# Row maxima of an 8192 x 8192 matrix: two rows a partition in each load, a finer tail, and a last store straight from the result tile

## The chip, the cores and the metric

One core of one Trainium2 chip. The metric is the device time in microseconds (us), the median of several executions. The profiled span is 1.84 us shorter than the measured time in the kernel before.

## The reference

```python
x = np.random.randn(8192, 8192).astype(np.float32)     # 268 MB
np.linalg.norm(x, ord=np.inf, axis=1)                  # max |x| of each row: 8192 results
```

Every byte is read once and little is computed, so the load stream sets the scale.

## The kernel before

A row block is 128 rows, one a partition. Each of 64 row blocks is loaded into one of five buffers and reduced on the vector engine (DVE). The last ten are cut into pieces whose partial maxima are combined by one more small reduction. At the end all results are transposed on the tensor engine (PE), copied out of the memory it writes to (PSUM) and stored.

```python
COOLDOWN = ([[4096, 4096]] * 7 + [[4096, 2048, 2048]]
            + [[2048] * 4] + [[2048, 2048, 1536, 1280, 1280]])
x_t = x.rearrange("(t p) m -> t p m", p=P)
pool = ctx.enter_context(tc.tile_pool(name="sbuf", bufs=5))
res = single.tile([P, T], mybir.dt.float32)
for t in range(T):
    xt = pool.tile([P, n_cols], x.dtype)
    for h, w in enumerate(chunks[t]):
        # ... dst is res[:, t] for a whole block, partial[:, h] for a piece
        nc.sync.dma_start(out=xt[:, off : off + w], in_=x_t[t, :, off : off + w])
        nc.vector.tensor_reduce(out=dst, in_=xt[:, off : off + w], axis=X,
                                op=max, apply_absolute_value=True)
    # ... if in pieces: tensor_reduce of partial[:, :n] into res[:, t]
nc.tensor.transpose(res_t_psum, res, ident)
nc.vector.tensor_copy(out=res_t, in_=res_t_psum)
nc.sync.dma_start(out=out.rearrange("(t p) -> t p", p=P), in_=res_t)   # 64 runs of 512 B
```

## Time and profile before

| | kernel before |
|---|---|
| time, median (range) | 634.71 us (634.56 to 634.78) |
| span | 632.9 us |
| loads, mean rate over the span | 80, 424 GB/s |
| vector engine busy | 88% |
| last byte of the input in | 626.4 us |
| last reduction ends | 629.3 us |
| last store: issued, issue to landing | 630.2, 1.8 us |

The prediction shows the lines for the rate, the end of the input and the last reduction. The last row is from the page's list of DMA issues (output and input, issuing queue, count, size of one, median us from issue to landing), followed by the wait of the sync queue at the end of the program (total, times, longest):

```profile
out_dram<-res_t SPq DMA_DIRECT2D x1, 32.0 KB, 1.8
```

```profile
SPq L107 <- DMA out_dram<-res_t: 1.1, 1, 1.1
```

### The profile page before, as it was taken

The page shows a single profiled execution, that of the slowest core. Times are in us where ns is not written, and L with a number is a line of the kernel's source. Part 1 is how long each engine was busy: PE and PEld are TensorE (multiplying, and loading weights), DVE is VectorE, ACT ScalarE, POOL GpSimd, SP SyncE. Part 2 cuts the span into 40 slices and gives each one's busy share as a digit, 9 for nine tenths or more (in the row PEclk, how much of TensorE's full clock was granted, in tenths as well). Part 3 has the DMA queues.
Part 4 walks back from the last instruction along what each step waited for, and adds up shares of the span by engine and source line. Part 5 has one row for each costly group of instructions (what it writes and reads, how often), then busy time and mean ns, then how long its engine had stood idle before and what let it go on. Part 6 is the DMA issues. An engine that isn't in the chain of part 4 may idle for free.

```text
span 632.9 us, 294 instructions
## 1 busy us (share of the span) xinstructions
PE 0.4 (0%) x1; PEld 0.1 (0%) x1; DVE 558.9 (88%) x91; POOL 0.7 (0%) x6
## 2 busy tenths in 40 slices
PE   0000000000000000000000000000000000000000
PEld 0000000000000000000000000000000000000000
DVE  1988988988989889889898898898988989999997
POOL 0000000000000000000000000000000000000000
DMA  8999999999999999999999999999999999999995
GB/s 373 439 437 437 433 431 433 431 431 431 431 431 431 431 431 431 431 431 431 431 431 431 431 431 431 431 431 431 431 437 433 435 435 418 427 428 431 425 421 219
DMA packets 11602, 268.49 MB, mean 424 GB/s; under 512 B 1296, under 2 KB 1360, under 8 KB 1744
## 3 DMA queue, kind: packets, MB, share of 16 engines
q1 hardware_dynamic: 11600, 268.47, 98.9%
q14 instruction: 2, 0.02, 0.0%
HBM read 268.44 MB, written 0.03 MB: 424 GB/s over the span
## 4 chain that ended last, share of the span: by engine, by line
DMA 75%; DVE 24%; SPq 0%; issue 0%; PE 0%; DVEq 0%
DMA xt<-in_x_dram 75%; DVE res L59 15%; DVE partial L59 8%; SPq L55 0%; DVE res L68 0%; PE res_t_psum L78 0%; DVE res_t L80 0%; DVEq L59 0%
## 5 line engine op out<-in xcount | busy, mean ns | idle before, releaser
L59 DVE TENSOR_REDUCE res<-xt 128x1 f32<-128x8192 f32 x54 | 469.0, 8686 | 67.6 <-DMA xt<-in_x_dram 67.6
L59 DVE TENSOR_REDUCE partial<-xt 128x1 f32<-128x4096 f32 (+3 forms) x26 | 88.1, 3430 | 2.7 <-DMA xt<-in_x_dram 2.6
L68 DVE TENSOR_REDUCE res<-partial 128x1 f32<-128x2 f32 (+3 forms) x10 | 1.6, 156 | 0.3
L80 DVE COPY res_t<-res_t_psum 64x128 f32<-64x128 f32 x1 | 0.3, 283 | 0.6 <-PE res_t_psum L78 0.6
L78 PE MATMUL res_t_psum<-ident,res 128*64 128x128 f32 x1 | 0.4, 393 | 629.5 <-DVE res L68 629.5
masks.py:199 POOL TENSOR_SCALAR_AFFINE_SELECT ident<-ident 128x128 f32<-128x128 f32 x1 | 0.3, 292 | 0.1
L78 PEld LDWEIGHTS res_t_psum<-ident,res 128*64 128x64 f32 x1 | 0.1, 128 | 629.4 <-issue 629.4
masks.py:197 POOL MEMSET ident<- 128x128 f32 x1 | 0.2, 204 | 0.3 <-POOLq L96 0.3
L96 POOL MEMSET const-bfloat16-1.0<- 128x1 bf16 x1 | 0.1, 101 | 0.0
L96 POOL MEMSET const-uint8-127<- 128x1 uint8 x1 | 0.1, 101 | 0.0
L96 POOL MEMSET const-float32-0.0<- 128x1 f32 x1 | 0.1, 98 | 0.2 <-issue 0.2
L96 POOL MEMSET const-float32-1.0<- 128x1 f32 x1 | 0.1, 98 | 0.0
## 6 DMA issues: line engine op xcount, KB each, us to landing
xt<-in_x_dram SPq DMA_DIRECT2D x54, 4096.0 KB, 39.8
xt<-in_x_dram SPq DMA_DIRECT2D x15, 2048.0 KB, 38.7
xt<-in_x_dram SPq DMA_DIRECT2D x8, 1024.0 KB, 28.3
xt<-in_x_dram SPq DMA_DIRECT2D x2, 640.0 KB, 17.9
xt<-in_x_dram SPq DMA_DIRECT2D x1, 768.0 KB, 19.3
out_dram<-res_t SPq DMA_DIRECT2D x1, 32.0 KB, 1.8
```

What stands on the lines that cost most here:

```text
L59: nc.vector.tensor_reduce(out=dst, in_=xt[:, off : off + w], axis=mybir.AxisListType.X, op=mybir.AluOpType.max, apply_absolute_value=True,)
L68: nc.vector.tensor_reduce(out=res[:, t : t + 1], in_=partial[:, : len(ch)], axis=mybir.AxisListType.X, op=mybir.AluOpType.max,)
L78: nc.tensor.transpose(res_t_psum, res, ident)
L80: nc.vector.tensor_copy(out=res_t, in_=res_t_psum)
L96: nc = _bacc.Bacc("TRN2", target_bir_lowering=False, num_devices=1)
```

## The change

The intent: fewer, larger loads where the stream is long (two rows of a partition are neighbours in memory, so a load moves 64 KB runs into a ring of columns); then pieces that shrink to 384 columns just as fast as the vector engine's lag may shrink, so that little is left when the last byte lands; the partial maxima lie behind the last piece in the ring, so that its reduction takes them along; and all results but the last 128 leave early, the last 128 without transpose and copy.

```diff
-    xt = pool.tile([P, n_cols], x.dtype)                 # five buffers of 8192 columns
+    ring = single.tile([P, RING + PAD], f32)             # RING = 3 * 16384 columns
+    x_big = x[:split].rearrange("(t p r) m -> t p (r m)", p=P, r=R)      # R = 2
+    for t in range(n_big):                               # 24 loads, 48 row blocks
+        nc.sync.dma_start(out=buf, in_=x_big[t])
+        absmax(res_big[:, t, :], buf.rearrange("p (r m) -> p r m", r=R))
+    for t, widths in enumerate(tail):                    # 16 row blocks; the last in 13 pieces
...
+            if i < n - 1:
+                absmax(ring[:, end + i : end + i + 1], ring[:, at : at + w])
+            else:
+                absmax(res_tail[:, t : t + 1], ring[:, at : at + w + n - 1])
+    store_early()                                        # all but the last 128, transposed
-    nc.tensor.transpose(res_t_psum, res, ident)
-    nc.vector.tensor_copy(out=res_t, in_=res_t_psum)
-    nc.sync.dma_start(out=out.rearrange("(t p) -> t p", p=P), in_=res_t)
+    nc.sync.dma_start(                                   # 128 runs of 4 B, side by side
+        out=out_tail[n_tail - 1].rearrange("(p o) -> p o", o=1),
+        in_=res_tail[:, n_tail - 1 : n_tail],
+    )
```

More of the change, by code (lines that the diff above doesn't have):

```diff
@@ L5, with tail_pieces @@
 import concourse.tile as tile
-from concourse import bass_utils, mybir
+from concourse import mybir
 from concourse.masks import make_identity
 from concourse._compat import with_exitstack
-COOLDOWN = (
-    [[4096, 4096]] * 7
-    + [[4096, 2048, 2048]]
-    + [[2048, 2048, 2048, 2048]]
-    + [[2048, 2048, 1536, 1280, 1280]]
-)
+P = 128
+R = 2
+RING = 3 * 16384
+PAD = 32
+LOAD = (1.1815e-3, 0.043)
+REDUCE = (1.0417e-3, 0.060)
+FIRST = 384
+GRAIN = 64
+def tail_pieces(n_cols, big):
+    slack = 0.0
+    lag = REDUCE[0] * FIRST + REDUCE[1]
+    rows = []
+    while True:
+        left, row = n_cols, []
+        while left:
+            w = FIRST if not rows and not row else int((lag + slack - REDUCE[1]) / REDUCE[0])
+            w = max(GRAIN, w // GRAIN * GRAIN)
+            if w >= left:
+                w = left
+            elif 2 * w > left:
+                w = (left // 2 + GRAIN - 1) // GRAIN * GRAIN
+            row.append(w)
+            left -= w
+            slack += (LOAD[0] - REDUCE[0]) * w + LOAD[1] - REDUCE[1]
+        rows.append(row[::-1])
+        if (lag + slack - REDUCE[1]) / REDUCE[0] > big:
+            return rows[::-1]
 @with_exitstack
@@ L26 @@
     nc = tc.nc
-    P = 128
+    f32 = mybir.dt.float32
     n_rows, n_cols = x.shape
-    assert n_rows % P == 0
-    T = n_rows // P
-    if n_cols == 8192 and T >= len(COOLDOWN):
-        chunks = [[n_cols]] * (T - len(COOLDOWN)) + COOLDOWN
-    else:
-        chunks = [[n_cols]] * T
-    x_t = x.rearrange("(t p) m -> t p m", p=P)
-    pool = ctx.enter_context(tc.tile_pool(name="sbuf", bufs=5))
-    single = ctx.enter_context(tc.tile_pool(name="single", bufs=1))
-    psum_pool = ctx.enter_context(tc.tile_pool(name="psum", bufs=1, space=bass.MemoryType.PSUM))
@@ L43 @@
-    res = single.tile([P, T], mybir.dt.float32)
-    maxch = max(len(c) for c in chunks)
-    if maxch > 1:
-        partial = single.tile([P, maxch], mybir.dt.float32)
-    for t in range(T):
-        ch = chunks[t]
-        assert sum(ch) == n_cols
-        xt = pool.tile([P, n_cols], x.dtype)
-        off = 0
-        for h, w in enumerate(ch):
-            dst = res[:, t : t + 1] if len(ch) == 1 else partial[:, h : h + 1]
-            nc.sync.dma_start(
-                out=xt[:, off : off + w],
-                in_=x_t[t, :, off : off + w],
-            )
-            nc.vector.tensor_reduce(
-                out=dst,
-                in_=xt[:, off : off + w],
-                axis=mybir.AxisListType.X,
-                op=mybir.AluOpType.max,
-                apply_absolute_value=True,
-            )
-            off += w
-        if len(ch) > 1:
-            nc.vector.tensor_reduce(
-                out=res[:, t : t + 1],
-                in_=partial[:, : len(ch)],
-                axis=mybir.AxisListType.X,
-                op=mybir.AluOpType.max,
-            )
@@ L75 @@
-    ident = single.tile([P, P], mybir.dt.float32)
-    make_identity(nc, ident)
-    res_t_psum = psum_pool.tile([T, P], mybir.dt.float32)
-    nc.tensor.transpose(res_t_psum, res, ident)
-    res_t = single.tile([T, P], mybir.dt.float32)
-    nc.vector.tensor_copy(out=res_t, in_=res_t_psum)
-    nc.sync.dma_start(out=out.rearrange("(t p) -> t p", p=P), in_=res_t)
+    tail = tail_pieces(n_cols, R * n_cols)
+    n_all = n_rows // P
+    if (n_all - len(tail)) % R:
+        tail.insert(0, [n_cols])
@@ new lines @@
+    n_big = (n_all - len(tail)) // R
+    n_tail = len(tail)
+    split = n_big * R * P
+    x_big = x[:split].rearrange("(t p r) m -> t p (r m)", p=P, r=R)
+    x_tail = x[split:].rearrange("(t p) m -> t p m", p=P)
+    out_tail = out[split:].rearrange("(t p) -> t p", p=P)
+    single = ctx.enter_context(tc.tile_pool(name="single", bufs=1))
+    psum_pool = ctx.enter_context(
+        tc.tile_pool(name="psum", bufs=1, space=bass.MemoryType.PSUM)
+    )
+    ring = single.tile([P, RING + PAD], f32)
@@ new lines, with room, absmax @@
+    ident = single.tile([P, P], f32)
+    res_big = single.tile([P, n_big, R], f32)
+    res_tail = single.tile([P, n_tail], f32)
+    make_identity(nc, ident)
+    head = 0
+    def room(w):
+        nonlocal head
+        if head + w > RING:
+            head = 0
+        at = head
+        head += w
+        return at
+    def absmax(dst, src):
+        nc.vector.tensor_reduce(
+            out=dst,
+            in_=src,
+            axis=mybir.AxisListType.X,
+            op=mybir.AluOpType.max,
+            apply_absolute_value=True,
+        )
@@ new lines, with store_early @@
+    for t in range(n_big):
+        at = room(R * n_cols)
+        buf = ring[:, at : at + R * n_cols]
+        nc.sync.dma_start(out=buf, in_=x_big[t])
+        absmax(res_big[:, t, :], buf.rearrange("p (r m) -> p r m", r=R))
+    def store_early():
+        line = single.tile([n_big, P, R], f32)
+        for r in range(R):
+            ps = psum_pool.tile([n_big, P], f32, name=f"ps{r}")
+            nc.tensor.transpose(ps, res_big[:, :, r], ident)
+            nc.scalar.copy(out=line[:, :, r], in_=ps)
+        nc.sync.dma_start(
+            out=out[:split].rearrange("(t q) -> t q", q=P * R),
+            in_=line.rearrange("t p r -> t (p r)"),
+        )
+        ps = psum_pool.tile([n_tail - 1, P], f32, name="ps_tail")
+        nc.tensor.transpose(ps, res_tail[:, : n_tail - 1], ident)
+        line_tail = single.tile([n_tail - 1, P], f32)
+        nc.scalar.copy(out=line_tail, in_=ps)
+        nc.sync.dma_start(out=out_tail[: n_tail - 1], in_=line_tail)
@@ new lines @@
+    for t, widths in enumerate(tail):
+        n = len(widths)
+        spots = [room(w) for w in widths[:-1]]
+        spots.append(room(widths[-1] + n - 1))
+        end = spots[-1] + widths[-1]
+        col = 0
+        for i, (w, at) in enumerate(zip(widths, spots)):
+            nc.sync.dma_start(out=ring[:, at : at + w], in_=x_tail[t, :, col : col + w])
+            col += w
+        for i, (w, at) in enumerate(zip(widths, spots)):
+            if i < n - 1:
+                absmax(ring[:, end + i : end + i + 1], ring[:, at : at + w])
+            else:
+                absmax(res_tail[:, t : t + 1], ring[:, at : at + w + n - 1])
@@ L85 @@
+    store_early()
+    nc.sync.dma_start(
+        out=out_tail[n_tail - 1].rearrange("(p o) -> p o", o=1),
+        in_=res_tail[:, n_tail - 1 : n_tail],
+    )
 _INS = ['x']
```

## The prediction

> **What bounds the kernel now.** I read the page first (slices, chain, groups, packets), then the timeline of the last 60 us, then the mean rates of five stretches, then the vector engine's and the sync queue's waits. The page:
>
> ```profile
> DMA  8999999999999999999999999999999999999995
> GB/s 373 439 437 437 433 431 433 431 431 431 431 431 431 431 431 431 431 431 431 431 431 431 431 431 431 431 431 431 431 437 433 435 435 418 427 428 431 425 421 219
> DMA packets 11602, 268.49 MB, mean 424 GB/s; under 512 B 1296, under 2 KB 1360, under 8 KB 1744
> ...
> DMA 75%; DVE 24%; SPq 0%; issue 0%; PE 0%; DVEq 0%
> ...
> L59 DVE TENSOR_REDUCE res<-xt 128x1 f32<-128x8192 f32 x54 | 469.0, 8686 | 67.6 <-DMA xt<-in_x_dram 67.6
> ```
>
> The 16 DMA engines are full from the first slice to the last but one. The vector engine is busy 88% and its idle time before the 54 whole-tile reductions ends on a load, 67.6 us in all. The chain gives it 24%, but only because a load that waits for a buffer is followed back through the reduction that freed it; the DMA row shows that such waits leave no hole. So the stream of loads is the bound, and only three things can shorten the run: the stream's rate, the start, and what follows the last load.
>
> The packet line says how rows move. There are 80 loads and one store; 81 x 16 = 1296 packets under 512 B, 16 small ones for each DMA, and 80 x 128 + 64 + 1296 = 11600, all of the load queue. So each 32 KB row run is one packet.
>
> The stretches (columns: window, its length, PE, PEld, DVE, POOL busy, clock, DMA share, GB/s):
>
> ```profile
> 13.00:538.00 525.00, 0.00 (x0) 0.00 (x0) 470.24 (x55) 0.00 (x0) 1.00 1.00 432
> 538.00:611.00 73.00, 0.00 (x0) 0.00 (x0) 70.06 (x25) 0.00 (x0) 1.00 1.01 426
> 611.00:625.20 14.20, 0.00 (x0) 0.00 (x0) 14.10 (x9) 0.00 (x0) 1.00 1.01 417
> 625.20:626.40 1.20, 0.00 (x0) 0.00 (x0) 1.20 (x2) 0.00 (x0) 1.00 0.12 47
> 626.40:629.30 2.90, 0.00 (x0) 0.00 (x0) 2.87 (x3) 0.00 (x0) 1.00 0.00 0
> 629.30:632.90 3.60, 0.39 (x1) 0.13 (x1) 0.31 (x2) 0.00 (x0) 1.00 0.04 9
> ```
>
> Runs of 32 KB stream at 432 GB/s, of 16 KB at 426, of 8 KB at 417: with the engines always full, shorter runs cost. The last byte is in at 626.4; then the vector engine works alone for 2.9 us, and 3.6 us of transpose, copy and store follow. The end in order of time:
>
> ```profile
> 582.50 4.42 DVE L59 TENSOR_REDUCE partial<-xt 128x1 f32<-128x4096 f32 x1 [0.35 <-DMA xt<-in_x_dram]
> ...
> 592.30 4.42 DVE L59 TENSOR_REDUCE partial<-xt 128x1 f32<-128x4096 f32 x1 [0.36 <-DMA xt<-in_x_dram]
> ...
> 602.09 8.81 DVE L59 TENSOR_REDUCE partial<-xt 128x1 f32<-128x4096 f32 x3 [0.35 <-DMA xt<-in_x_dram]
> ...
> 629.17 0.16 DVE L68 TENSOR_REDUCE res<-partial 128x1 f32<-128x5 f32 x1
> ...
> 629.47 0.39 PE L78 MATMUL res_t_psum<-ident,res 128*64 128x128 f32 x1 [629.47 <-DVE res L68]
> 629.90 0.28 DVE L80 COPY res_t<-res_t_psum 64x128 f32<-64x128 f32 x1 [0.58 <-PE res_t_psum L78]
> 630.21 0.55 SPq L81 DMA_DIRECT2D out_dram<-res_t  x1
> ```
>
> A tile of two 4096-column pieces takes 592.30 - 582.50 = 9.80 us (9.79 for its neighbours). Whole tiles start at 12.88 and, the 54th, at 527.99: 515.11 / 53 = 9.719 us. After 602.09 no wait on a load is listed: the last three tiles are reduced without a pause, so the vector engine falls behind the stream.
>
> **The Trainium skill.** (1) "DMA: Bandwidth & Descriptors", section "Where 436 GB/s comes from", gives a ceiling of 435.2 GB/s. The trace agrees: 432 in the long stretch. There is under 1% to win in rate. (2) The same page, "Why small descriptors are slow (HBM only)": each packet and each descriptor carries a fixed overhead. The fall from 432 through 426 to 417 agrees, though the page speaks of far smaller descriptors. (3) "VectorE: DVE Perf Modes", "The perf-mode tier table": tensor_reduce has only the 1x mode; at that page's 0.96 GHz 8192 columns are 8.53 us, and the trace has 8.686, so about 0.15 us is fixed. (4) The DMA page's "Specifications" asks for at least 512 B in a transfer, with read-modify-write below. The new last store has 4 B runs; nothing before shows its cost.
>
> **The change, part by part.**
>
> *Loads.* Cost of an extra load at equal bytes: 9.795 - 9.719 = 0.076 us (eight more row packets and one small packet on each engine). Then a whole tile is 9.643 us of bytes plus 0.076. That is 435.0 GB/s without the overhead, at the ceiling, which makes me trust the split. I take it as linear in the number of loads. Before: 54 + 14 + 3 + 4 + 5 = 80. After, by the instruction order of the changed kernel: 24 of 16384 columns (two rows for each partition, 64 KB runs), 8 of 8192, 8 of 4096, then 3, 4, 6 and 13 pieces: 66. So 14 x 0.076 = 1.06 us less: 24 fewer by the long runs (-1.8), 10 more in the finer tail (+0.8). The last byte lands at 626.4 - 1.1 = 625.3.
>
> *Buffers.* Three slots of 16384 columns in place of five of 8192. A slot is free 17.2 us after its load landed (16384 / 0.96 + 0.15); issue 0.33 us and about 1.3 us to first data (the first load: issued at 0.74, moving from 2.1). A load takes 19.36 us and another whole one is queued, so the engines don't run dry: the margin is one load.
>
> *Backlog.* When the first 8192-column tile lands, 9.72 us after the last large one, the vector engine still has 17.1 - 9.7 = 7.4 us to do. Back to back a reduction takes w / 0.96 + 0.06 us (pieces of 2048 start 2.195 us apart), 8.59 for a tile; it gains 1.13 a tile and is level after seven. The pieces that follow shrink at the speed at which the lag may shrink: stepping through all 66 with these two costs, the last 384-column piece finds the engine free or at most 0.1 us late.
>
> *The end.* Before, 632.87 - 626.4 = 6.5 us. After: wake 0.02, reduction of 384 columns and 12 partials 396 / 0.96 = 0.41 plus 0.15, wake 0.03, store issue to landing 1.8 (the old store's median), landing to end of span 632.87 - (630.21 + 1.8) = 0.86. That is 3.3 us: 3.2 less. Gone from the path are the 2.9 us of lag (0.6 stay), the separate combining reduction, the transpose and the copy. The early results' transposes, ScalarE copies and two stores wait for the row block before the last, some 10.6 us before the end (8192 columns plus 13 loads' overhead), and lie beside the loads.
>
> *Sum.* -1.06 - 3.2 = -4.3 us. I give back 0.4 as an estimate for two things that no row prices: 4 B runs in the last store, and pieces of 1.5 to 3 KB runs, whose packets may cost more than the linear term. -3.9 us: span 629.0; the time lies 634.71 - 632.87 = 1.84 above the span: 630.8.
>
> **The rivals.**
> - *The 64 KB runs gain nothing*, since they move as two packets. For it: nothing before has a run over 32 KB. Against it: runs of 8, 16 and 32 KB each went as one packet. It takes back 1.7 us: 632.5.
> - *The small pieces starve the queue.* The changed order makes every load wait for the one eight before it; an issue takes 0.33 us, and a 384-column piece moves in 0.45 + 0.08 us. Against it: the last seven pieces are 3392 columns, 4.5 us of stream, and landing, waking, issue and first data need about 2.7. If it happens, +0.5 to 1.5 us: 631.3 to 632.3.
> - *The vector engine's lag survives*, because small reductions cost more than 0.06 apart. For it: where a reduction waits for its load the whole 0.15 counts. With 30 pieces and 0.05 more each, 1.5 us: 632.3.
> - *The rate rises above the linear term.* All load overhead is 66 x 0.076 = 5.0 us; without any of it the time would be 625.8, 1.4% under before. So faster by over 2%, 622.0, is out of reach by this model.
> - *Three slots are too few*, with holes in the DMA row at each 19.4 us: a hole of 1 us for each of 21 waits would add 21 us. The margin above speaks against it.
>
> **Range and chances.** The centre is 630.8. Both of the first two rivals together give about 633; a dearer last store belongs inside too. Below, a cheaper long run gives perhaps 1 us. Range 629.5 to 632.8. Within 2%: 0.97; faster 0.01; slower 0.02, for a stall that I don't see.
>
> **What would show it.** Packets: 66 x 128 + 24 + 15 + 128 rows and about 16 for each DMA, some 9,700 (12,800 if long runs are split). GB/s near 433.5 in the long stretch. Large reductions of about 17.2 us, starting 19.36 apart. Last byte near 625.3; last reduction ended 0.6 later; from there 2.7 us to the end. I am wrong if the DMA row shows holes after the start, if reductions run without a wait over the last 10 us, or if the last store takes over 2.5 us.

## The result, and the profile after

| | before | after | predicted |
|---|---|---|---|
| time, median | 634.63 us (the runs above and one more) | 636.66 us (636.48 to 636.89) | 630.8 (629.5 to 632.8) |
| span | 632.9 | 634.7 | 629.0 |
| large reductions apart | - | 19.35 | 19.36 |
| packets of the load queue | 11600 | 9714 | some 9,700 |
| last packet of the loads ends | 626.4 | 625.3 | 625.3 |
| last reduction ends | 629.3 | 626.5 | 625.9 |
| last store, issue to landing | 1.8 | 7.2 | 1.8 |

The ratio is 1.0031 (95% interval 1.0017 to 1.0045). Ratios here are the mean time of one kernel's fast runs over that of the other's of the same rounds, so they are not quite the ratio of the medians quoted. The change is slower by 2 us where 4 us less were predicted; the time lies outside the range. The differences discussed are about 1% at most.

The page of the changed kernel:

```profile
DMA  9999999999999999999999999999999999999993
...
DMA packets 9716, 268.49 MB, mean 423 GB/s; under 512 B 1227, under 2 KB 1778, under 8 KB 3954
...
L92 DVE TENSOR_REDUCE res_big<-ring 128x2 f32<-128x16384 f32 x24 | 413.3, 17220 | 71.6 <-DMA ring<-in_x_dram 71.6
```

No hole in the DMA row, one packet for each 64 KB run (else there would be 3072 more), and the large reduction at the expected 17.2 us. Two of them from the timeline, 19.34 us apart:

```profile
41.92 17.22 DVE L92 TENSOR_REDUCE res_big<-ring 128x2 f32<-128x16384 f32 x1 [2.13 <-DMA ring<-in_x_dram]
61.26 17.22 DVE L92 TENSOR_REDUCE res_big<-ring 128x2 f32<-128x16384 f32 x1 [2.12 <-DMA ring<-in_x_dram]
```

Stretches (same columns as in the prediction, with ScalarE, ACT, ahead of POOL):

```profile
23.00:470.00 447.00, 0.00 (x0) 0.00 (x0) 397.98 (x24) 0.00 (x0) 0.00 (x0) 1.00 1.00 433
470.00:615.00 145.00, 0.59 (x2) 0.13 (x2) 143.84 (x29) 0.47 (x2) 0.00 (x0) 1.00 1.00 427
615.00:624.90 9.90, 0.40 (x1) 0.10 (x1) 9.74 (x13) 0.25 (x1) 0.00 (x0) 1.00 0.99 372
624.90:625.70 0.80, 0.00 (x0) 0.00 (x0) 0.80 (x2) 0.00 (x0) 0.00 (x0) 1.00 0.06 20
625.70:626.50 0.80, 0.00 (x0) 0.00 (x0) 0.74 (x2) 0.00 (x0) 0.00 (x0) 1.00 0.00 0
626.50:634.70 8.20, 0.00 (x0) 0.00 (x0) 0.00 (x0) 0.00 (x0) 0.00 (x0) 1.00 0.01 0
```

The last line is the find: 8.2 us in which no engine works and next to nothing moves. In order of time, the last lines of the timeline (start, us, engine, line, what), then the DMA issue and the sync queue's wait:

```profile
616.51 9.36 DVE L92 TENSOR_REDUCE ring<-ring 128x1 f32<-128x768 f32 x12
625.91 0.57 DVE L92 TENSOR_REDUCE res_tail<-ring 128x1 f32<-128x396 f32 x1
```

```profile
626.50 0.36 SPq L139 DMA_DIRECT2D out_dram<-res_tail  x1
```

```profile
out_dram<-line_tail SPq DMA_DIRECT2D x1, 7.5 KB, 3.9
out_dram<-res_tail SPq DMA_DIRECT2D x1, 0.5 KB, 7.2
```

```profile
SPq L166 <- DMA out_dram<-res_tail: 6.8, 1, 6.8
```

The last reduction ended 2.8 us earlier than before, and the store of 0.5 KB then took 7.2 us where 32 KB had taken 1.8. The chain of waits is no help: it is followed back from the last counted instruction, the reduction that ended at 626.5, so it does not contain the 8.2 us after it. Compare the span's end with the last instruction's end first.

The trace has more on this store. Its packets were all moved between 627.4 and 627.6 us; but the 16 DMA engines' reports that their part has landed came one after another from 629.9 to 633.7 us. In the kernel before the 16 reports came within 0.2 us.

### The profile page after: what moved, and what is told of

Same layout as the page of the kernel before. It is cut to its first block, busy times and chain, and to the rows that moved or that the text cites. A ratio compares the mean times of both kernels' runs of the same rounds, so it can differ in the third digit from the quotient of the medians.

```text
span 634.7 us, 247 instructions
## 1 busy us (share of the span) xinstructions
PE 1.0 (0%) x3; PEld 0.2 (0%) x3; DVE 553.5 (87%) x66; ACT 2.0 (0%) x4; POOL 0.7 (0%) x6
## 3 DMA queue, kind: packets, MB, share of 16 engines
q1 hardware_dynamic: 9714, 268.47, 98.4%
## 4 chain that ended last, share of the span: by engine, by line
DMA 65%; DVE 33%; another core or an unknown queue 0%; issue 0%; SPq 0%; DVEq 0%
DMA ring<-in_x_dram 65%; DVE res_big L92 24%; DVE res_tail L92 6%; DVE ring L92 2%; SPq L103 0%; DVEq L92 0%
## 5 line engine op out<-in xcount | busy, mean ns | idle before, releaser
L92 DVE TENSOR_REDUCE res_big<-ring 128x2 f32<-128x16384 f32 x24 | 413.3, 17220 | 71.6 <-DMA ring<-in_x_dram 71.6
L92 DVE TENSOR_REDUCE res_tail<-ring 128x1 f32<-128x8192 f32 (+5 forms) x16 | 94.6, 5946 | 1.2 <-DMA ring<-in_x_dram 1.0
L92 DVE TENSOR_REDUCE ring<-ring 128x1 f32<-128x4096 f32 (+15 forms) x26 | 46.4, 1831 | 0.1
```

The source lines that it names most:

```text
L92: nc.vector.tensor_reduce(out=dst, in_=src, axis=mybir.AxisListType.X, op=mybir.AluOpType.max, apply_absolute_value=True,)
```

## The experiments

My theory was that the 4 B runs of the last store cost the time and that the rest of the change works as predicted. The rivals were that the loss lies in the long runs or the small pieces, or that the end of the stream is slow for any store. Fifteen kernels ran.

**end_pe**: the changed kernel, the last 128 results transposed into one row.

```diff
-    nc.sync.dma_start(out=out_tail[n_tail - 1].rearrange("(p o) -> p o", o=1), in_=res_tail[:, n_tail - 1 : n_tail])
+    nc.tensor.transpose(ps, res_tail[:, n_tail - 1 : n_tail], ident)
+    nc.vector.tensor_copy(out=line_last, in_=ps)
+    nc.sync.dma_start(out=out_tail[n_tail - 1 : n_tail], in_=line_last)     # one run of 512 B
```

> The changed kernel, but the last 128 results are transposed on PE into one row, copied, and stored as one 512 B run. Theory (the 4 B runs of the last store cost the time: 7.2 us from issue to landing against 1.8): PE and copy put about 0.9 us back on the path, the store falls by 5.4, so -4.5 us against the changed kernel: 632.1 us, ratio to before 0.996. Rival (the loss lies in the long runs or the small pieces, and the store's late landing only reflects a DMA system that is slow at the end): the store still lands late, 636 to 638 us, ratio about 1.003.

Measured 631.5 us against 634.84, ratio 0.9947 (0.9935 to 0.996), correct. Its end:

```profile
626.30 0.57 DVE L92 TENSOR_REDUCE res_tail<-ring 128x1 f32<-128x396 f32 x1
626.92 0.08 PEld L140 LDWEIGHTS ps_last<-ident,res_tail 128*1 128x1 f32 x1 [9.95 <-DVE res_tail L92]
626.93 0.37 PE L140 MATMUL ps_last<-ident,res_tail 128*1 128x128 f32 x1 [9.66 <-DVE res_tail L92]
627.34 0.28 DVE L142 COPY line_last<-ps_last 1x128 f32<-1x128 f32 x1 [0.47 <-PE ps_last L140]
627.64 0.23 SPq L143 DMA_DIRECT2D out_dram<-line_last  x1
```

The detour costs 0.8 us (626.87 to 627.64), and the span ends at 629.7, 2.1 us after the issue in place of 8.2. (The time is 0.6 us under the expectation: by the trace the single run of 512 B landed 1.1 us after its issue, not 1.8.) Undoing this one part turns a loss into a gain.

**before_direct**: the kernel before, with only this part of the change.

```diff
-    nc.tensor.transpose(res_t_psum, res, ident)          # all 64 columns, copied, stored
+    # 63 columns transposed, copied on ScalarE and stored; then
+    nc.sync.dma_start(out=out_t[T - 1].rearrange("(p o) -> p o", o=1), in_=res[:, T - 1 : T])
```

> The kernel before with this one part of the change: 63 row blocks' results transposed and stored first, the last 128 straight from the result tile as 4 B runs. Theory: the last store lands 7.2 us after issue in place of 1.8, and the transpose and copy (0.75 us) leave the path: 634.6 + 5.4 - 0.75 = 639.3 us, ratio 1.007. Rival (4 B runs are slow only behind the small loads of the changed tail): store near 2 us, 634.0 us, ratio 0.999.

Measured 639.94 us against 634.84, ratio 1.0081 (1.0068 to 1.0095), correct.

```profile
out_dram<-res SPq DMA_DIRECT2D x1, 0.5 KB, 7.4
```

So the long landing comes with this store wherever it stands. The small loads ahead of it have no part in it: in this kernel the last load had landed over 2 us before the store was issued.

**end_dve**: the vector engine transposes in 32x32 blocks; four partitions store 128 B runs.

```diff
+    nc.vector.transpose(out=last32_t, in_=last32)        # last result is column 0 of last32
+    nc.sync.dma_start(out=out_tail[n_tail - 1].rearrange("(b j) -> b j", j=32), in_=last32_t[0:P:32, :])
```

> The changed kernel, but the last reduction writes a column of a 128x32 tile, the vector engine transposes it in 32x32 blocks, and four partitions store 128 B runs. Theory (the cost goes with the number of small writes): four runs, landing about 2 us after issue, transpose about 0.2 us: 636.66 - 5.2 + 0.25 = 631.7 us, ratio 0.9954. Rival (any run under 512 B pays a long landing): landing stays 5 us or more, 634 us or above.

Measured 631.68 us against 634.84, ratio 0.9951 (0.9939 to 0.9964), correct. The transpose took 0.21 us, but the issue of the store 0.62 us in place of 0.23, and the span ends 2.7 us after it began, at 629.9: as good as PE, not better. Four runs of 128 B are not slow, so it is not every run under 512 B.

**before_long**: the kernel before, with only the long runs, for the first 54 row blocks.

```diff
+    for t in range(n_big):                               # 27 loads of 16384 columns, ring of three
+        nc.sync.dma_start(out=buf, in_=x_big[t])
+        # ... one reduction of (2, 8192) columns into res_big[:, t, :]
     # the ten row blocks of COOLDOWN as before
```

> The kernel before with the long runs alone: 27 loads of two rows a partition (64 KB runs) for the first 54 row blocks, same tail of ten, same end. Theory: 27 loads fewer at 0.076 us is 2.05 us: 632.6 us, ratio 0.9968, large loads 19.35 us apart. The large reductions leave a lag of 8 us that must be worked off in ten row blocks; the last three of before are already without a wait, so up to 0.5 us may come back. Rival (long runs gain nothing or cost): 634.6 or above, ratio 1.000 or more.

Measured 637.9 us against 634.84, ratio 1.0049 (1.0035 to 1.0063), correct: slower, against my theory. The trace says why. Timeline and stretches:

```profile
526.19 17.22 DVE L57 TENSOR_REDUCE res_big<-ring 128x2 f32<-128x16384 f32 x1 [2.14 <-DMA ring<-in_x_dram]
543.33 8.73 DVE L78 TENSOR_REDUCE partial<-ring 128x1 f32<-128x4096 f32 x2
...
633.18 0.16 DVE L87 TENSOR_REDUCE res<-partial 128x1 f32<-128x5 f32 x1
```

```profile
624.00:625.00 1.00, 0.00 (x0) 0.00 (x0) 0.94 (x2) 0.00 (x0) 0.00 (x0) 1.00 0.08 31
625.00:633.00 8.00, 0.00 (x0) 0.00 (x0) 8.00 (x5) 0.00 (x0) 0.00 (x0) 1.00 0.00 0
```

The last packet of the loads ended at 624.9 us, 1.5 us earlier than before, where 2 were promised. But after 526.19 the vector engine never waits again: it has 17.2 us of the last large reduction and 90.0 us of ten row blocks to do (543.33 to 633.34), while the stream brings those ten blocks in 98.4 (ten at 9.72 us, and 16 more pieces at 0.076). It ends about 8 us behind. In the kernel before the same sum starts with 8.7 in place of 17.2. I had counted the lag and misjudged how fast it shrinks: a block in pieces with its combining reduction takes 8.97 us, so it gains 0.8 us, not 1.13. Long runs with the old tail are a loss here; with the longer tail of the change, eight whole blocks first and no combining reduction, they gain (end_pe_r1 below).

**end_pe_r1**: end_pe with 48 loads of one row a partition in place of 24 of two, same tail.

```diff
-R = 2
+R = 1        # tail_pieces still called with 2 * n_cols, so the tail stays
```

> The version with the last store transposed on PE, but with the first 48 row blocks in 48 loads of one row a partition (32 KB runs) in place of 24 of two; the tail of 16 row blocks and the end stay. By the cost of 0.076 us a load, 24 more loads cost 1.8 us: 631.5 + 1.8 = 633.3 us, ratio 0.9976 to before. Rival (long runs gain nothing here): 631.5 us, ratio 0.9947.

Measured 632.85 us against 634.77, ratio 0.9973 (0.996 to 0.9985), correct. With the tail that suits them, the long runs are worth 0.9973 / 0.9947, 0.26% or 1.7 us; 24 loads at 0.076 us were 1.8. The two stood in different calls, so this compares their ratios to before; the intervals just touch at 0.996, the times do not overlap (632.8 us and more here, 631.7 and less in end_pe). What is left of the gain, 1.7 us, comes with the tail, its early store and the ring, which were not separated.

**end_pe_1280**: end_pe with a last piece of 1280 columns.

```diff
-FIRST = 384
+FIRST = 1280     # 54 loads in place of 66
```

> The version with the last store transposed on PE, but with a last piece of 1280 columns in place of 384, so 54 loads in place of 66. By the terms of the prediction: 12 loads fewer are 0.9 us less of stream, the last reduction is 0.9 us longer: the same, 631.5 us, ratio 0.9947. If the small pieces stream worse than the linear term (the last ones have runs of 1.5 to 3 KB): 0.3 to 0.6 us faster. If the small pieces are what brings the gain at the end: 632.4 us.

Measured 631.18 us against 634.77, ratio 0.9944 (0.9931 to 0.9958), correct: the same as end_pe. The last reduction ended at 626.79 us in this trace and at 626.87 in that of end_pe: what the shorter last reduction saves, the extra loads cost. The 384-column pieces bring nothing over 1280.

The next kernels vary only the last store of the changed kernel. Their outputs are wrong, which doesn't matter for the times. The quantity is the store's time from issue to landing, from one profile each. In all but rows32 and rows127 the store of 15 rows ahead of it is left out, because the last store takes its place in the output. No run leaves it out and keeps the 128 results side by side, so its share in the 7.2 us is not isolated; but in end_pe, with it, the last store was quick, and in before_direct, where the store ahead was issued 8 us earlier (621.53 and 629.80 us), the last one was slow.

**stride64**: 4 B each, 64 B apart.

```diff
-        out=out_tail[n_tail - 1].rearrange("(p o) -> p o", o=1),
+        out=out[split:].rearrange("(p s) -> p s", p=P)[:, 0:1],
```

> The changed kernel with its last 128 results of 4 B stored 64 B apart in place of side by side (wrong result on purpose; the 15-row store, whose place it takes, is left out). In the changed kernel the store took 7.2 us from issue to landing. Theory E (each DMA engine finishes its own 8 small writes one after the other, (7.2 - 1.1) / 8 = 0.76 us each): unchanged, about 7.2 us. Theory G (all 128 pass one common place, 0.05 us each): unchanged, about 7.2 us. Theory L (small writes into the same short stretch of memory wait for one another): about 2 to 3 us.

```profile
out_dram<-res_tail SPq DMA_DIRECT2D x1, 0.5 KB, 1.5
```

The same 128 writes of 4 B from the same tile land in 1.5 us. This clears the size of the run and rules out a cost per small write, in the engine (E) or in a common place (G). The same writes are slow when they lie side by side.

**runs64**: 128 runs of 64 B, side by side, 8 KB.

```diff
+        out=out[split:].rearrange("(p s) -> p s", p=P),
+        in_=res_tail,
```

> The changed kernel with a last store of 128 runs of 64 B (16 results each, all of the tail; wrong order on purpose, the 15-row store left out). Theories E and G, if the cost is that of any run under 512 B: about 7.2 us from issue to landing, since the count of runs is the same. Theory L, or a cost of 4 B writes alone: 2 to 3 us.

```profile
out_dram<-res_tail SPq DMA_DIRECT2D x1, 8.0 KB, 1.5
```

Sixteen times the bytes, and as quick.

**rows32** and **rows127**: fewer results, 4 B side by side.

```diff
+        out=out_tail[n_tail - 1, :32].rearrange("(p o) -> p o", o=1),      # rows127: :127
+        in_=res_tail[:32, n_tail - 1 : n_tail],
```

> The changed kernel with the last store cut to its first 32 results (the other 96 are left unwritten, wrong on purpose), 4 B side by side, two on each of 16 engines. Theory E: 1.1 + 2 x 0.76 = 2.6 us to landing. Theory G: 1.1 + 32 x 0.05 = 2.7 us. Theory L with stretches of 64 B (16 results): each stretch has as many writers as before, about 7 us; with one stretch of 512 B: 2.7 us.

> The changed kernel with the last store cut to 127 results (one left unwritten, wrong on purpose), which puts all of them on one DMA engine. Theory E: 127 x 0.76 + 1.1, about 98 us to landing. Theory G: about 7.2 us. Theory L: [...]either about 7 us or, if waiting comes only from different engines meeting, 2 to 3 us.

The store of 32 landed in 3.1 us:

```profile
out_dram<-res_tail SPq DMA_DIRECT2D x1, 0.1 KB, 3.1
```

For the 127 the page gives no landing time. They did go through one engine: the trace has one report after their packets had moved, where the 128 have 16. The sync queue's wait for the store:

```profile
SPq L168 <- DMA out_dram<-res_tail: 8.1, 1, 8.1
```

That is 8.1 us, as against 6.8 for 128 results on 16 engines. So it needs no different engines that meet, and spreading the writes over 16 engines gains little. The 32 results are over 1.5 us by 1.6, the 128 by 5.7: about 0.05 us for each result both times, although both have 16 results in each 64 B. If each 64 B were held up by itself and beside the others, 32 would have taken as long as 128.

**stride16**, **stride8** and **runs16**: how far apart is far enough.

```diff
+        out=out[split : split + 4 * P].rearrange("(p s) -> p s", p=P)[:, 0:1],   # stride16; stride8: 2 * P
+        out=out[split : split + 4 * P].rearrange("(p s) -> p s", p=P),           # runs16, of res_tail[:, n_tail - 4 :]
```

> The changed kernel with its last 128 results of 4 B stored 16 B apart (wrong result on purpose). Side by side they took 7.2 us to land, 64 B apart 1.5 us. If writes within the same 64 B wait for one another, four share a stretch here and landing lies between: with every write but the first of a stretch held up by 0.05 us, 1.5 + 96 x 0.05 = 6 us; if stretches go beside each other, about 1.7 us. If the unit is 16 B or less: 1.5 us.

> The changed kernel with its last 128 results of 4 B stored 8 B apart (wrong result on purpose). Landing so far: 7.2 us side by side, 2.0 at 16 B apart, 1.5 at 64 B apart. If writes within the same 16 B are taken one after the other in one common place (96 such followers cost 5.7 us, so 0.06 us each), 64 followers give 1.5 + 3.8 = 5.3 us. If what counts is how many writes lie in a longer stretch (64 B: 16, then 4 at 16 B apart), 8 to a stretch should give something near 3 us.

> The changed kernel with a last store of 128 runs of 16 B side by side, 2 KB in all (wrong order on purpose). If 16 B is the unit, no two writes share one: 1.5 to 2.0 us, as for 4 B writes 16 B apart. If any short writes that lie side by side in 64 B hold each other up, four to a stretch: 2 us if it goes by the number in a stretch, over 4 us if it goes by touching neighbours.

| last store | runs in each 64 B of output | issue to landing |
|---|---|---|
| 4 B side by side (changed kernel) | 16 | 7.2 us |
| 4 B, 8 B apart | 8 | 3.3 |
| 4 B, 16 B apart | 4 | 2.0 |
| 16 B side by side | 4 | 2.5 |
| 4 B, 64 B apart | 1 | 1.5 |
| 64 B side by side | 1 | 1.5 |

The 16 B unit falls: it asked for 5.3 us at 8 B apart, and 3.3 was measured, near the 3 us of a count over a longer stretch. The 16 B runs side by side, at 2.5 us, lie between their two forecasts (2, and over 4). The excess over 1.5 us goes 5.7, 1.8, 0.5 as the distance doubles, so it falls faster than the number in a stretch. With rows32 no simple rule of mine gives all the rows. Shown is that crowding of runs is the cost and that at 64 B apart it is gone; the unit (nothing was run at 32 B) and the mechanism stay open. With 128 runs a larger distance also means a longer piece of output, 512 B to 8 KB, and these runs do not tell the two apart.

**tail_pt**: the finding put to use, in a correct kernel. The last 16 row blocks are dealt out so that a partition has 16 rows in succession. Then its 16 results are 64 B of output in one piece, and the tail needs no transpose at all.

```diff
-    x_tail = x[split:].rearrange("(t p) m -> t p m", p=P)
-    out_tail = out[split:].rearrange("(t p) -> t p", p=P)
+    x_tail = x[split:].rearrange("(p t) m -> t p m", p=P)
+    out_tail = out[split:].rearrange("(p t) -> p t", p=P)
...
+    nc.sync.dma_start(out=out_tail, in_=res_tail)        # the only store of the tail
```

> A correct kernel that uses what the wrong-on-purpose stores showed: the changed kernel, but the last 16 row blocks are dealt out so that a partition holds 16 rows that follow one another in memory, and all their results leave in one last store of 128 runs of 64 B straight from the result tile, with no transpose. Theory (only small writes side by side are slow): store lands 1.5 us after issue, 630.9 us, ratio 0.994. Rival (rows 512 KB apart on the load side slow the last 16 row blocks): GB/s in the last quarter falls well below 430 and the time exceeds 632 us.

Measured 631.1 us against 634.77, ratio 0.9942 (0.993 to 0.9954), correct. The store lands in 1.5 us, and the stretch from 470 to 590 us still streams at 428 GB/s (428 in stride16, whose tail is dealt out as in the change), so rows 512 KB apart do not slow the loads.

**tail_pt_1280**: both together.

```diff
-FIRST = 384          # tail_pt
+FIRST = 1280
```

> The two best versions joined: one last store of 64 B runs straight from the result tile, and a last piece of 1280 columns (54 loads). The end with the transpose gave 631.2 with it and 631.5 without; so 630.7 us, ratio 0.9936, if the parts add up; 631.1 if the piece size makes no difference.

Measured 630.55 us against 634.83, ratio 0.9932 (0.9918 to 0.9945), correct. Its median is the lowest of all, 4.3 us below the kernel before and, by the ratios, about 1.0% below the changed kernel. Its interval overlaps that of tail_pt and end_pe; between those it is not decided.

## Why the prediction was wrong

**The step that failed** is one term of the sum for the end: "store issue to landing 1.8 (the old store's median)". It carried the duration of a store of 64 runs of 512 B over to one of 128 runs of 4 B. It measured 7.2 us, 5.4 more. The prediction had noted that "nothing before shows its cost" and gave back 0.4 us as an estimate for this and the small pieces together; the 5.4 missing here is more than the whole predicted gain of 3.9. That end_pe, without this store, gains 3.3 us, and that before_direct, with this store and without the rest of the change, loses 5.1, shows that this term turned the sign. A part with no row in the profile should have widened the range, not been priced by its neighbour. The prediction did name the sign: it called itself wrong "if the last store takes over 2.5 us". That the time stayed within 2%, as it had given a chance of 0.97, says nothing for its sum: all its terms are small.

The account closes: span predicted 629.0, measured 634.7. The store is 5.4, the last reduction ended 0.6 late (626.5, predicted 625.9), the way from landing to the end of the span 0.1 (1.0 in place of 0.86), and the allowance of 0.4 is to be taken off: 5.7.

**A second term, the wake after the last load**, was also too small. The prediction started the last reduction 0.02 us after the last byte. The last packet ended at 625.3 us, as predicted (625.7 in end_pe, with the same loads). But the last load counts as landed only 5.3 us after its issue at 620.46, which the trace puts at 625.75, and the reduction began at 625.91. The issue from the timeline, then the time to landing from the view of the tile `ring` in a window that holds this load alone:

```profile
620.46 0.33 SPq L131 DMA_DIRECT2D ring<-in_x_dram  x1
```

```profile
DMA to landing us min/median/max: 5.3/5.3/5.3
```

So of the 0.6 us some 0.45 lie between the last packet and the landing, and 0.15 behind the reduction before. In the kernel before this time was hidden: its vector engine was still busy with earlier pieces.

**Loads**: right. Large loads 19.35 us apart (19.36), 9714 packets (some 9,700), and the long runs alone worth 1.7 us (1.8) in end_pe_r1. The rival that they gain nothing is refuted there.

**Buffers**: right. Three slots leave no hole in the DMA row.

**Backlog**: right for the changed kernel. The timeline lists few waits on loads in the tail (1.0 us in three, for reductions into the result tile) and none in the last 10 us, which the prediction had called a sign of being wrong. The sign was badly chosen: from 618 to 625.4 us the trace has each reduction that can be matched begin 0.02 to 0.07 us after its own load landed (landed 622.91 and begun 622.93, 623.59 and 623.61), so the engine was level with the stream; its records overlap by up to 0.09 us, and no gap is left to list. It was a nearer thing than I wrote: before_long shows a loss of 3 us where the tail doesn't fit the larger loads.

**Small pieces**: the queue did not starve. The last 10 us streamed at 372 GB/s, and yet the last packet ended at 625.3 us, as the linear cost of 0.076 us a load had it. The 2.7 us that the prediction set against starving came without a working, and no run tests it by itself. That the pieces pay for themselves was assumed; end_pe_1280 shows that they break even.

**The end**: the lag, the combining reduction, the transpose and the copy did leave the path. The last reduction ended 2.8 us earlier, and the store was issued 3.7 us earlier (626.50 against 630.21). The store took it all back, and 1.7 more.

## What to carry to other kernels

A transpose and a copy ahead of a store can be the cheap part: 0.8 us here, against 5.7 for storing one column as neighbouring 4 B runs. Where the layout may be chosen, deal the rows out so that each partition owns 64 B of successive output, as tail_pt does; there the store needed no transpose and landed in 1.5 us. And when a load is made larger, add up the work that the reducing engine has left when the last large one lands, and compare it with the stream that is still to come.

## What the Trainium skill lacked or had wrong

- "DMA: Bandwidth & Descriptors", section "Specifications", asks for 512 B or more in a transfer and names read-modify-write below. For a last store of 128 runs the length alone made no difference here: runs of 4 B that lie 64 B apart and runs of 64 B both landed in 1.5 us, the 64 runs of 512 B of the kernel before in 1.8. What it lacks is that crowding costs: 4 B runs side by side took 7.2 us, 8 B apart 3.3, 16 B apart 2.0.
- The same page, section "Why small descriptors are slow (HBM only)", speaks of small descriptors. It lacks a cost at large runs: 433 GB/s with 64 KB runs, 432 with 32 KB, 426 with mostly 16 KB, 417 with 8 KB and less, or about 0.07 us for each load of 128 runs.
